# Moving the gathering tiles' scores ahead of the last four projections, and two tiles' routing beside them

## The chip, the cores and the metric

The kernel runs on one core of a Trainium2 chip. Its time is the device time of one execution in microseconds (us), taken as the median of several runs. Engines are named as the profile names them: PE is TensorE (PEld its weight loads), DVE is VectorE, ACT is ScalarE, POOL is GpSimd, SP is SyncE, whose queue issues most transfers.

## The reference, cut to what matters

One layer of an encoder over 1024 tokens of width 1024. A mixer (latent attention and a Hyena convolution) gives `mix`; after a layer norm, a PEER block picks 16 of 16384 experts for each of 8 heads of each token and sums their rows, weighted:

```
mix = concat([a, y]) @ w_o
h = layer_norm(ALPHA * h + mix)
# peer_ffn, for each chunk xc of 128 tokens:
q = (xc @ w_q).reshape(C, 8, 2, 64)
s = einsum('chpd,hpnd->chpn', q, sub_keys)       # 2 x 128 scores a head
sv, si = top_k(s, 16)                            # each half's best 16
cand = sv[:, :, 0, :, None] + sv[:, :, 1, None, :]
best, pos = top_k(cand, 16)                      # best 16 of their sums
eidx = take_along_axis(cidx, pos)                # expert numbers
g = softmax(best)
a = gelu(einsum('chkd,cd->chk', u_tab[eidx], xc))
f = einsum('chk,chkd->cd', g * a, v_tab[eidx])
h = layer_norm(ALPHA * h + f)
```

## The kernel before, in words

The 1024 tokens are 8 tiles of 128. The first NG = 3 tiles are gathering tiles: for them GpSimd fetches the chosen rows of both tables with indirect transfers, row by row (`gather`, L1233), and VectorE multiplies and sums them. The other DENSE = 5 tiles are dense tiles: TensorE multiplies them with the whole tables, 128 blocks of 128 experts, and a matrix of gates, built on chip (`build_g`), zeroes the experts that were not chosen.

The stages around the change, in program order:

- `mix(tt)` (L945) projects tile tt with `w_o`: ScalarE and VectorE split the operand into a high and a low half (`zh`, `zl`; two pairs of buffers, `first` and `second`), TensorE does 48 matmuls into two PSUM banks, VectorE adds the residual and normalises, and the tile is stored in `h2_d`. For the gathering tiles `transposed` puts the transposed halves in `hg` as soon as the next tile is projected.
- `scores(src, t0, nt)` (L971) makes the scores of nt tiles, head by head: the head's weight block `wr` and keys are loaded and split, TensorE projects (24 matmuls for each cut of the columns; the dense tiles have two cuts of 320) and multiplies with the keys, ScalarE copies, and `s_d` gets the result. It yields after each head.
- Before the change all 8 tiles are projected first. Then the gathering tiles' scores run, with the load and transposes of one dense tile (`hd`) after each of the first five heads; then the dense scores, with two pieces of `route(0)` after each head.
- `route(tt, rp, done)` (L1015) picks the experts of one tile from its scores. It is VectorE work, but for one Exp on ScalarE, in 11 pieces, and starts with a load of all of the tile's scores, `r_s` (L1019), into a pool whose tiles have one buffer each.
- The early u loop does 72 parts (`u_part`): 48 matmuls each on the dense tiles, an activation and a store in `a_d`. Its program also draws on `weights()`, a generator that yields the remaining routes and the five `build_g`: `route(NG)`, then each dense tile's `build_g` with the next tile's route beside it, then what is left. How much it draws for each part is set by `total`, and `tick` adds the gather's steps by a fixed rate.
- The main loop does the other 56 u parts, all v blocks and the rest of the gather.

What order the instructions take on each engine is planned when the kernel is built, with a simulated timeline (`schedule_with_timeline_sim=True` in `kernel`); each engine then works through its list in that order. `tc.issue_after(ins)` puts what is traced in its block behind `ins` on that engine. Pools opened with `side="right"` or `"left"` form two stacks in SBUF; a tile in a reopened space waits until the old tile's last reader is done.

Of the kernel before, what the change touches and what calls it, by code (L numbers as in the profile page):

```python
# [10 lines left out]
F32 = mybir.dt.float32  # L11
F32R = mybir.dt.float32r
# [9 lines left out]
P = 128  # L22
T = 1024
D = 1024
NT = T // P
ND = D // P
# [4 lines left out]
DENSE = 5  # L31
# [258 lines left out]
def split(nc, hi, lo, src):  # L290
    nc.scalar.copy(hi, src)  # L291
    return nc.vector.tensor_sub(lo, src, hi)  # L292
# [3 lines left out]
def layer(ctx: ExitStack, tc: tile.TileContext, a: dict, out: bass.AP):  # L296
    nc = tc.nc
    TD = DENSE * P
    NG = NT - DENSE
# [40 lines left out]
    def transposed(src, hi, lo, c0):  # L340

        for q in range(0, ND, 4):
            ps = psO.tile([P, 4, P], F32, name=f"ps_o{q // 4}")
            for ct in range(4):
                nc.tensor.transpose(ps[:, ct], src[:, (q + ct) * P:(q + ct + 1) * P], ident)
            r = split(nc, hi[:, q:q + 4, c0:c0 + P], lo[:, q:q + 4, c0:c0 + P], ps)
        return r

    s_mix = ExitStack()
# [525 lines left out]
    h2_d = dram.tile([NT, P, D], F32, name="h2_d")  # L875
    s_d = dram.tile([NT, P, 8, 256], F32, name="s_d")
    s_wo = ExitStack()
# [22 lines left out]
    n_h, n_a, done = 32, 72, 0  # L900
# [27 lines left out]
    s_q = ExitStack()  # L928
# [14 lines left out]
    normed = []  # L943
# [69 lines left out]
    CHUNK = 55.0 / 12  # L1013
# [96 lines left out]
    s_e = ExitStack()  # L1110
    with tc.tile_pool(name="hgp", bufs=1, side="right") as hgp:
        hg = hgp.tile([P, 2, ND, TG], F32R, name="hg")
        turn = None
        for tt in range(NT):
            m_t = mix(tt)
            if turn is not None:
                transposed(turn, hg[:, 0], hg[:, 1], (tt - 1) * P)
            turn = m_t if tt < NG else None
        s_wo.close()
        s_mix.close()  # L1120
        hdp = s_e.enter_context(tc.tile_pool(name="hdp", bufs=1, side="left"))
        hd = hdp.tile([P, 2, ND, TD], F32R, name="hd")
        with tc.tile_pool(name="hrp", bufs=2, side="left") as hrp:
            gs = scores(hg, 0, NG)
            for t in range(DENSE):
                next(gs)
                h_t = hrp.tile([P, D], F32, name="h_t")
                nc.sync.dma_start(h_t, h2_d[NG + t])
                transposed(h_t, hd[:, 0], hd[:, 1], t * P)
            for _ in gs:  # L1130
                pass


    CS = 32
# [3 lines left out]
    NB = 4  # L1138
    HOT = 0.69
# [155 lines left out]
    def tick(cost):  # L1295
        pace["credit"] += cost
        while pace["credit"] >= pace["step"]:
            pace["credit"] -= pace["step"]
            next(ga, None)
# [2 lines left out]
    n_steps = NG * (2 * P + GB)  # L1302
    pace["step"] = EARLY * UC / (n_steps * EHEAD)

    with tc.tile_pool(name="rp", bufs=1, side="left") as rp, \
            tc.tile_pool(name="gp", bufs=1, side="left") as gp:
        base = gp.tile([98, P], F32, name="base")
        own = gp.tile([98, 32], F32, name="own")
        nc.sync.dma_start(base, a["par_base"])
        nc.sync.dma_start(own, a["par_own"])  # L1310
        par_r = gp.tile([98, 32, P], BF16, name="par_r")
        nc.vector.tensor_mul(par_r, base.unsqueeze(1).to_broadcast([98, 32, P]),
                             own.unsqueeze(2).to_broadcast([98, 32, P]))
        jls = [gp.tile([98, 4, P], BF16, name=f"jl{i}") for i in range(2)]
        for jl in jls:
            nc.gpsimd.memset(jl[96:98], 1.0)
        r0 = route(0, rp, [])
        for _ in scores(hd, NG, DENSE):
            with tc.issue_after(normed[-1].ins):
                for _ in range(2):  # L1320
                    next(r0, None)
        for _ in r0:
            pass
        s_q.close()
        gap = s_e.enter_context(tc.tile_pool(name="gap", bufs=2, side="right"))

        def weights():


            done = []  # L1330
            yield from route(NG, rp, done)
            for t in range(DENSE):
                beside = route(NG + t + 1, rp, done) if t + 1 < DENSE else route(1, rp, done)
                for n, c in enumerate(build_g(done[t], t, gp)):
                    yield c
                    if n % 5 in (0, 2, 4):
                        yield next(beside, 0.0)
                yield from beside
            for g in range(2, NG):
                yield from route(g, rp, done)  # L1340

        gw = weights()
        total = (NT - 1) * 12 * CHUNK + TD // NB * HOT
        done = 0.0
        for e in range(EARLY):
            while done < (e + 1) * total / GFILL:
                c = next(gw, None)
                if c is None:
                    break
                done += c  # L1350
            A = u_part(e, u_early)
            nc.scalar.dma_start(a_d[e], A)
            tick(UC)
        for _ in gw:
            pass
# [199 lines left out]
```

## Time and profile before

| | |
|---|---|
| time, median of 3 runs | 3274.26 us (3264.43 to 3280.19) |
| the profiled execution's own time | 3255.75 us |
| its span in the profile | 3254.0 us |
| PE busy | 2988.5 us (92%) |
| DVE busy | 2735.7 us (84%) |
| ACT busy | 1256.2 us (39%) |
| POOL busy | 1036.4 us (32%) |
| mean granted clock of PE | 0.962 |

Busy times are sums over the whole span, and stages differ. The granted clock is a share of full speed: 1.00 is 2.4 GHz, and a lower mean is a mix of 2.4 and 1.2 GHz. Matmuls are pipelined, so the duration of one is longer than the distance to the next. The profiled execution is shorter than all three timed runs.

### The profile page before, as it was taken

The numbers are of one execution on the slowest core, as the hardware profiler recorded it, in microseconds if no ns is written. First come the engines' busy times: TensorE is split into PE (matmuls) and PEld (weight loads), VectorE is DVE, ScalarE is ACT, GpSimd is POOL, SyncE is SP. The second block draws the span as 40 slices with busy tenths as digits, with TensorE's granted clock in tenths as the row PEclk, the third lists the DMA queues.
The fourth block names the chain that finished last, engine by engine and source line by source line (L and its number), as shares of the span: only waits on it lengthen the run. The fifth ranks groups of instructions, "written<-read, shape, count | busy, mean of one in ns | idle before, by whom it ended". The sixth has DMA issues, their size and how long they took to land.

```text
span 3254.0 us, 44798 instructions
## 1 busy us (share of the span) xinstructions
PE 2988.5 (92%) x15582; PEld 2552.1 (78%) x15582; DVE 2735.7 (84%) x5514; ACT 1256.2 (39%) x2454; POOL 1036.4 (32%) x797
## 2 busy tenths in 40 slices
PE   6999898889999779999999789998999999799997
PEld 5677676556689778999898778886888888588886
DVE  7556799888757799999999768888889879888888
ACT  4544344455523216766574122222222222122222
POOL 0000000000000351332435735555555445455551
PEclk9999889989999989999999899999999999999998
DMA  5244743322444777887888999999999999989995
GB/s 173 97 149 133 249 123 104 102 56 73 138 152 149 278 252 241 302 303 277 310 284 319 364 338 336 325 358 341 329 358 323 353 315 333 337 302 353 342 332 188
DMA packets 355064, 828.87 MB, mean 255 GB/s; under 512 B 34345, under 2 KB 144851, under 8 KB 351253
## 3 DMA queue, kind: packets, MB, share of 16 engines
q0 software_dynamic: 110592, 402.70, 34.5%
q1 hardware_dynamic: 230709, 356.71, 33.9%
q10 hardware_dynamic: 13536, 66.59, 5.2%
q8 instruction: 123, 2.02, 0.2%
q14 instruction: 104, 0.85, 0.1%
HBM read 715.52 MB, written 110.33 MB: 254 GB/s over the span
## 4 chain that ended last, share of the span: by engine, by line
PE 31%; DVE 22%; DMA 7%; issue 6%; POOL 3%; ACT 1%; SPq 0%; DVEq 0%; POOLq 0%; ACTq 0%
PE ps_x L285 5%; PE ps_x L287 5%; PE ps_x L286 5%; DVE grow L1262 4%; DVE gacc L1270 4%; DMA vr<-in_peer_v 3%; PE ps_h L285 3%; PE ps_h L287 3%; PE ps_h L286 3%; POOL grow L1249 3%; DVE p L1160 2%; PE ps_o L285 2%; PE ps_o L286 2%; PE ps_o L287 2%; DVE ul L292 2%
## 5 line engine op out<-in xcount | busy, mean ns | idle before, releaser
L1249 POOL DMA_INDIRECT grow<-in_peer_u,eid x384 | 518.0, 1349 | 582.3 <-DVE grow L1262 206.9
L1249 POOL DMA_INDIRECT grow<-in_peer_v,eid x384 | 504.8, 1315 | 606.1 <-DVE gacc L1270 267.3
L1270 DVE SCALAR_TENSOR_TENSOR gacc<-grow,dot,gacc 128x1024 f32<-128x1024 f32 x381 | 487.3, 1279 | 13.2 <-DMA grow<-in_peer_v,eid 9.6
L1262 DVE SCALAR_TENSOR_TENSOR grow<-grow,gh 128x1024 f32<-128x1024 f32 x384 | 460.1, 1218 | 19.8 <-DMA grow<-in_peer_u,eid 19.5
L287 PE MATMUL ps_x<-hd,ul 128*128 128x320 f32 x1152 | 368.3, 328 | 50.1 <-DVE ul L292 49.7
L285 PE MATMUL ps_x<-hd,uh 128*128 128x320 f32 x1152 | 373.6, 325 | 28.4 <-ACT uh L291 26.2
L286 PE MATMUL ps_x<-hd,uh 128*128 128x320 f32 x1152 | 370.3, 322 | 0.0
L286 PE MATMUL ps_x<-vl,wh 128*128 128x512 f32 x864 | 341.1, 395 | 1.7 <-DVE vl L292 1.6
L287 PE MATMUL ps_x<-vh,wl 128*128 128x512 f32 x864 | 336.8, 393 | 0.0
L285 PE MATMUL ps_x<-vh,wh 128*128 128x512 f32 x864 | 302.3, 396 | 28.4 <-ACT vh L291 23.2
L291 ACT CAST vh<-vr 128x512 fp32r<-128x512 f32 x256 | 156.3, 619 | 388.4 <-DMA vr<-in_peer_v 280.6
L285 PE MATMUL ps_h<-hd,uh 128*128 128x320 f32 x896 | 278.8, 311 | 9.0 <-ACT A L1221 5.6
L286 PE MATMUL ps_h<-hd,uh 128*128 128x320 f32 x896 | 278.3, 311 | 0.0
L287 PE MATMUL ps_h<-hd,ul 128*128 128x320 f32 x896 | 275.8, 311 | 2.5 <-DVE ul L292 2.5
L287 PEld LDWEIGHTS ps_x<-hd,ul 128*128 128x128 f32 x1152 | 222.7, 195 | 65.0 <-DVE ul L292 59.0
L285 PEld LDWEIGHTS ps_x<-hd,uh 128*128 128x128 f32 x1152 | 225.9, 196 | 35.4 <-ACT uh L291 31.8
L292 DVE TENSOR_TENSOR vl<-vr,vh 128x512 fp32r<-128x512 f32 x256 | 174.5, 687 | 75.7 <-ACT vh L291 74.4
L286 PEld LDWEIGHTS ps_x<-hd,uh 128*128 128x128 f32 x1152 | 225.8, 196 | 0.8
L291 ACT CAST uh<-ur 128x1024 fp32r<-128x1024 f32 x128 | 134.7, 1052 | 223.7 <-DMA ur<-in_peer_uT 103.1
L285 PEld LDWEIGHTS ps_x<-vh,wh 128*128 128x128 f32 x864 | 162.7, 190 | 63.5 <-ACT vh L291 24.7
L292 DVE TENSOR_TENSOR ul<-ur,uh 128x1024 fp32r<-128x1024 f32 x128 | 155.5, 1215 | 63.8 <-ACT uh L291 62.4
L286 PEld LDWEIGHTS ps_x<-vl,wh 128*128 128x128 f32 x864 | 164.4, 190 | 37.1 <-DVE vl L292 4.4
(366 smaller groups left out, 6876.3 us busy)
## 6 DMA issues: line engine op xcount, KB each, us to landing
ur<-in_peer_uT SPq DMA_DIRECT2D x128, 512.0 KB
vr<-in_peer_v SPq DMA_DIRECT2D x256, 256.0 KB
g_d<-gst ACTq DMA_DIRECT2D x20, 2048.0 KB
gt<-g_d SPq DMA_DIRECT2D x32, 1280.0 KB
a_d<-A ACTq DMA_DIRECT2D x72, 320.0 KB
A<-a_d SPq DMA_DIRECT2D x72, 320.0 KB
fw<-in_dft_fw SPq DMA_DIRECT2D x64, 256.0 KB
wr<-in_w_in SPq DMA_DIRECT2D x16, 512.0 KB
```

The lines of the kernel that those rows point to most:

```text
L285: nc.tensor.matmul(out, L[0], R[0], start=start, stop=False)
L286: nc.tensor.matmul(out, L[0], R[1], start=False, stop=False)
L287: return nc.tensor.matmul(out, L[1], R[0], start=False, stop=stop)
L291: nc.scalar.copy(hi, src)
L292: return nc.vector.tensor_sub(lo, src, hi)
L1160: nc.vector.tensor_tensor(p1, iota.unsqueeze(1).to_broadcast([P, NB, P]), ig[:, 0, c:c + NB].unsqueeze(2).to_broadcast([P, NB, P]), op=ALU ...
L1249: nc_i = nc.gpsimd.indirect_dma_start(out=t, out_offset=None, in_=a["peer_" + kind], in_offset=bass.IndirectOffsetOnAxis(ap=eid[g][:, k:k ...
L1262: nc.vector.scalar_tensor_tensor(t, t, 1.0, h_t, op0=ALU.mult, op1=ALU.mult, accum_out=d[:, k - k0:k - k0 + 1])
L1270: nc.vector.scalar_tensor_tensor(acc, t, dots[k0][:, k - k0:k - k0 + 1], acc, op0=ALU.mult, op1=ALU.add)
```

## The change

The gathering tiles' scores are made as soon as four tiles are projected. Then a pool `rp0` is opened on the right, in the space that `hg` leaves, and two routes, of tiles 0 and 1, are chained in one generator, `r0`. Two of its pieces are traced after each of the four projections that are left, one after the transposes of each dense tile, and two after each head of the dense scores; there are 22 in all. The dense transposes no longer have the gathering scores between them. `weights()` has route(2) where route(1) was, and `total` counts one route less. The pools `rp` and `gp`, and the table `par_r`, now come after the dense scores.

```diff
-        for tt in range(NT):
+        for tt in range(NG + 1):
             m_t = mix(tt)
             if turn is not None:
                 transposed(turn, hg[:, 0], hg[:, 1], (tt - 1) * P)
-            turn = m_t if tt < NG else None
-        s_wo.close()
-        s_mix.close()
-        hdp = s_e.enter_context(tc.tile_pool(name="hdp", bufs=1, side="left"))
-        hd = hdp.tile([P, 2, ND, TD], F32R, name="hd")
-        with tc.tile_pool(name="hrp", bufs=2, side="left") as hrp:
-            gs = scores(hg, 0, NG)
-            for t in range(DENSE):
-                next(gs)
-                h_t = hrp.tile([P, D], F32, name="h_t")
-                nc.sync.dma_start(h_t, h2_d[NG + t])
-                transposed(h_t, hd[:, 0], hd[:, 1], t * P)
-            for _ in gs:
-                pass
+            turn = m_t
+        for _ in scores(hg, 0, NG):
+            pass
+    rp0 = s_q.enter_context(tc.tile_pool(name="rp0", bufs=1, side="right"))
+    r0 = (c for g in range(2) for c in route(g, rp0, []))
+    for tt in range(NG + 1, NT):
+        mix(tt)
+        for _ in range(2):
+            next(r0)
+    s_wo.close()
+    s_mix.close()
+    hdp = s_e.enter_context(tc.tile_pool(name="hdp", bufs=1, side="left"))
+    hd = hdp.tile([P, 2, ND, TD], F32R, name="hd")
+    with tc.tile_pool(name="hrp", bufs=2, side="left") as hrp:
+        for t in range(DENSE):
+            h_t = hrp.tile([P, D], F32, name="h_t")
+            nc.sync.dma_start(h_t, h2_d[NG + t])
+            transposed(h_t, hd[:, 0], hd[:, 1], t * P)
+            next(r0, None)
...
+    for _ in scores(hd, NG, DENSE):
+        with tc.issue_after(normed[-1].ins):
+            for _ in range(2):
+                next(r0, None)
+    for _ in r0:
+        pass
+    s_q.close()
+    gap = s_e.enter_context(tc.tile_pool(name="gap", bufs=2, side="right"))
     with tc.tile_pool(name="rp", bufs=1, side="left") as rp, \
             tc.tile_pool(name="gp", bufs=1, side="left") as gp:
...
-        r0 = route(0, rp, [])
-        for _ in scores(hd, NG, DENSE):
-            with tc.issue_after(normed[-1].ins):
-                for _ in range(2):
-                    next(r0, None)
-        for _ in r0:
-            pass
-        s_q.close()
-        gap = s_e.enter_context(tc.tile_pool(name="gap", bufs=2, side="right"))
...
-                beside = route(NG + t + 1, rp, done) if t + 1 < DENSE else route(1, rp, done)
+                beside = route(NG + t + 1, rp, done) if t + 1 < DENSE else route(2, rp, done)
...
-            for g in range(2, NG):
+            for g in range(3, NG):
                 yield from route(g, rp, done)
...
-        total = (NT - 1) * 12 * CHUNK + TD // NB * HOT
+        total = (NT - 2) * 12 * CHUNK + TD // NB * HOT
```

## Rows read from the trace of the kernel before

**Rows 1.** The page: span, and busy time of each engine.

```profile
span 3254.0 us, 44798 instructions
PE 2988.5 (92%) x15582; PEld 2552.1 (78%) x15582; DVE 2735.7 (84%) x5514; ACT 1256.2 (39%) x2454; POOL 1036.4 (32%) x797
```

**Rows 2.** Busy time by stage: stretch, length, engines, granted clock, DMA share, GB/s.

```profile
897.00:940.00 43.00, 43.00 (x196) 35.72 (x195) 26.22 (x39) 4.74 (x10) 0.00 (x0) 1.00 0.24 86
940.00:992.00 52.00, 52.00 (x310) 50.67 (x310) 22.58 (x26) 24.45 (x43) 0.99 (x2) 1.00 0.67 222
992.00:1067.00 75.00, 73.54 (x461) 70.74 (x460) 55.59 (x233) 26.36 (x51) 0.00 (x0) 1.00 0.39 125
1067.00:1250.00 183.00, 139.31 (x842) 134.36 (x841) 173.85 (x664) 45.57 (x83) 79.49 (x58) 0.89 0.77 264
1250.00:1750.00 500.00, 475.48 (x3356) 456.24 (x3355) 497.31 (x1448) 326.49 (x900) 163.58 (x129) 0.98 0.83 293
1750.00:1838.00 88.00, 73.24 (x460) 69.05 (x459) 72.98 (x79) 24.71 (x54) 56.42 (x40) 0.94 0.94 355
1838.00:3254.00 1416.00, 1332.16 (x6759) 1160.83 (x6757) 1203.67 (x1623) 365.30 (x603) 723.30 (x542) 0.98 0.93 328
```

**Rows 3.** TensorE's timeline, 938 to 952: start, length, instruction.

```profile
939.58 0.40 PE L287 MATMUL ps_x<-wo,zl 128*128 128x512 f32 x1
...
945.88 1.04 PE L345 MATMUL ps_o<-ident,h_t 128*128 128x128 f32 x8
```

**Rows 4.** Busy time by stage of L1221, two halves a u part.

```profile
1067.00:1250.00 183.00, 18.78 (x37) 0.89 0.77 264
1250.00:1750.00 500.00, 44.07 (x89) 0.98 0.83 293
1750.00:1838.00 88.00, 7.08 (x17) 0.94 0.94 355
```

**Rows 5.** Waits in 1067 to 1670: total us, times, longest.

```profile
PE ps_x L287 <- DVE ul L292: 43.5, 15, 7.3
```

**Rows 6.** VectorE's timeline, 990 to 1072; in brackets the idle time before.

```profile
992.41 4.43 DVE L1312 TENSOR_TENSOR par_r<-base,own 98x4096 bf16<-98x4096 f32 x1 [3.85 <-DMA own<-in_par_own]
...
1001.83 1.26 DVE L1023 MAX8 r_sv<-r_s 128x8 f32<-128x128 f32 x6 [3.86 <-DMA r_s<-s_d]
...
1017.29 1.21 DVE L292 TENSOR_TENSOR wl<-wr,wh 128x1024 fp32r<-128x1024 f32 x1
...
1051.98 0.23 DVE L1078 CAST eid<-r_ef 128x128 int32<-128x128 f32 x1
1071.62 1.23 DVE L292 TENSOR_TENSOR ul<-ur,uh 128x1024 fp32r<-128x1024 f32 x1 [19.42 <-ACT uh L291]
```

**Rows 7.** VectorE's instruction groups, 1001 to 1053: busy us, mean ns.

```profile
L292 DVE TENSOR_TENSOR wl<-wr,wh 128x1024 fp32r<-128x1024 f32 x5 | 6.1, 1215 | 0.0
```

**Rows 8.** ScalarE's timeline, 940 to 1090.

```profile
1004.19 1.05 ACT L291 CAST wh<-wr 128x1024 fp32r<-128x1024 f32 x1 [1.94 <-PE ps_x L286]
```

**Rows 9.** The chain that ended last, 985 to 1110.

```profile
993.65 0.38 ACT sc L999
994.05 2.75 DMA s_d<-sc
996.86 4.95 DMA r_s<-s_d
```

**Rows 10.** SP's timeline of issued transfers, 855 to 1140.

```profile
940.05 0.80 SPq L1128 DMA_DIRECT2D h_t<-h_d  x2
...
996.86 0.33 SPq L1019 DMA_DIRECT2D r_s<-s_d  x1
```

**Rows 11.** TensorE's instruction groups, 860 to 1067: busy us, mean ns.

```profile
L345 PE MATMUL ps_o<-ident,h_t 128*128 128x128 f32 x40 | 5.2, 273 | 0.0
```

**Rows 12.** TensorE's timeline, 1300 to 1322: two matmuls in a row.

```profile
1299.96 0.31 PE L287 MATMUL ps_x<-hd,ul 128*128 128x320 f32 x1
1300.11 0.31 PE L285 MATMUL ps_x<-hd,uh 128*128 128x320 f32 x1
```

## The prediction

> **What bounds the kernel now.** I read the page's busy shares first [rows 1]: TensorE 92%, VectorE 84% of 3254.0 us. An average over unlike stages decides nothing, so the table by stage comes next [rows 2]. I chose its cuts from the timelines: 897–940 is the projection of the last four tiles (its last matmul is at 939.58 [rows 3]); 940–992 the gathering tiles' scores with the dense tiles' transposes between them; 992–1067 the dense scores with route(0) beside them; 1067–1838 the early u loop, whose 72 parts write two halves each (143 of 144 lie in it [rows 4]), with the other seven routes, build_g and the gather's first steps; 1838–3254 the main loop.
>
> The reader should see two things. Up to 1067 TensorE is full: 43.0 of 43, 52.0 of 52, 73.5 of 75 us, while VectorE has room: 26.2, 22.6 and 55.6 us. From 1067 it turns round: VectorE is busy 744.1 us of 771 (173.85 + 497.31 + 72.98, 96.5%), TensorE 688.0 (89%). In 1250–1750 they stand at 497.3 and 475.5 of 500. The waits of the early loop say the same: matmuls wait 43.5 us for the low half of a u block, which VectorE makes [rows 5]. The main loop holds no instruction that changes and moves as a whole with what comes ahead of it.
>
> **Part 1: one route leaves the early loop.** Before, route(1) and route(2) lie in it beside five dense routes; after, only route(2). Route(0) shows the price: its first instruction starts at 1001.83, its last ends at 1052.21 [rows 6], and in these 50.4 us stand five weight splits of 6.1 us [rows 7]: 44.3 us, or 4.03 for each of its 11 pieces. `total` falls with it, so the rest is still spread over the loop.
>
> How much is the loop shortened by 44.3 us less VectorE work? At VectorE's present share of 96.5% the other 699.8 us take 725 us: a gain of 46. At that length TensorE's 688 us would be 95%, as high as it stands now in 1250–1750. This is the upper end. For the lower end I let TensorE hold the middle: the outer stretches (271 of 771 us) take their part of the saving, 44.3 × 271/771 = 15.6 us, and the middle gains half of TensorE's 24.5 idle us, 12.3: together 28. I take 38, a little above the midpoint of 37, since TensorE at 733 us is at 94%, not above what the middle shows already.
>
> A page speaks on this room. The row first: in 1250–1750 weight loads are busy 456.2 us, 91.2%, against 50.67 of 52 (97.4%) where matmuls run back to back in 940–992 [rows 2]. The Trainium skill, Perfetto Trace Analysis, section Identifying the Most-Contended Engine, says to judge TensorE by weight-load share, not by matmul time. By it the middle's room would be an estimated 500 × (1 − 0.912/0.974) = 32 us, and the lower end 31 instead of 28.
>
> **Part 2: routes 0 and 1 beside the last four projections.** TensorE's instructions are the same; only their order and cover change. Two pieces follow each of four mixes: 8 pieces, 32.2 us, where VectorE has 43 − 26.2 = 16.8 us free. What is queued behind them on VectorE: the next tile's splits, then its residual add, which frees the PSUM banks; TensorE waits for both. A queue of this kind is there already: a weight block's cast ends at 1005.24 and its split starts only at 1017.29, 12 us later, behind route pieces that the program emits first [rows 8, 6]. There TensorE had other heads to do and lost 1.5 us in 75. So the upper end is 32.2 − 16.8 = 15 us; the lower end is 0, because two operand pairs and four banks let TensorE run a tile (43/4 = 10.8 us) ahead. I take 8, midway.
>
> The route also starts later than TensorE's next tile: from the last score copy at 993.65 the store takes 2.75 and the load 4.95 us until VectorE starts at 1001.83, 8.2 us [rows 9]. The load waits in SP's queue for that store [rows 10]; behind it stand the projections' h_t loads and h2_d stores, which have a tile's lead over 8.2 us. I cost this at nothing; without the lead it is 8.2 us, about half of the 15. The second load waits for route(0)'s last read of its one buffer; behind it stand dense weight loads with two buffers, cost nothing, the bound again one landing, 5 us. The gathering scores' 8 weight loads, 16 key loads and 8 stores move past four mixes' loads and stores on SP; in 897–940 transfers hold 24% of the engines [rows 2], so they find room. Exp in a route needs ScalarE, 26.4 of 75 us busy beside the dense scores: nothing. The 4.43 us par_r product [rows 6] moves behind the dense scores; VectorE stands idle 19.42 us ahead of 1071.62 [rows 6], which hides it; without that it is 4.4 us. GpSimd's first gather still waits for the end of the scores.
>
> **Part 3: the dense transposes lose their cover.** This is what is late next. The second mix tail is not new, but in 940–992 the gathering scores filled it: TensorE 52.0 of 52. After the change those scores are done by then. The first two h_t loads go out at 940.05, with the last matmul of the projections, and the first transposes run at 945.88 [rows 10, 3]: 5.8 us. Two buffers for five tiles make three turns. Tiles 0 to 2, which the first half of a head's columns needs, are in place after about 5.8 + 1.0 + 5.8 us and a transpose and its split, some 16 us, of which TensorE works 3 (40 transposes took 5.2 us [rows 11]): 13 lost. While the last tiles come, two heads' first halves (24 matmuls at 0.147 us [rows 12], 3.5 us each) fill in. With landings of 4 us (between the 2.75 and 4.95 of [rows 9]) it is 10: the lower end. The upper end adds route pieces that stand ahead of the splits, 4 × 4.03 = 16 more: 29. I take 15, near the unburdened chain, since VectorE has free time while the loads land.
>
> **Part 4: the clock.** The granted clock is 1.00 (2.4 GHz) in all of 897–1067, where TensorE never rests, and 0.89, a mix of 2.4 and 1.2 GHz, in 1067–1250, where it idles 43.7 us [rows 2]. There 0.11 × 183 = 20 us of full speed go with 43.7 idle, 0.46 for each; by the same ratio 13 idle us cost 6. Lower end 0; I take 3. The Trainium skill, TensorE: Matmul & The Clock Gate, section HAM oscillation, has the rule that speaks against this change: after a gap TensorE's clock is cut and the next matmuls start slow. By that rule the sum would be 3 us worse than the one below, by an unmoved clock 3 better; the low clock of 1067–1250 agrees with the rule.
>
> **Sum.** −38 + 8 + 15 + 3 = −12 us. The profiled execution took 3255.75 us, so 3244 by its own time. It lies 18.5 us below the median of 3274.26 (three runs, 3264.43 to 3280.19), so against the median: 3262. The ends: −46 + 10 = −36 and −28 + 15 + 29 + 6 = +22. A difference of 0.5%, 16.4 us, is about what a measurement of this kernel can tell from none.
>
> **The rivals.**
> *The routes hide* (chance 0.22). The pieces run in VectorE's idle time, as they do beside the dense scores, where 44.3 us of route cost TensorE 1.5. Front 10, loop −46: −36, 3238. For it: VectorE has 16.8 + 19.4 free us and the order on each engine is planned when the kernel is built. Against it: two routes are 88.6 us, and from the gathering scores' end TensorE has 43 + 5 + 75 = 123 us left, of which the route loses 8.2 to the landing and VectorE gives 26 to the mixes and more to the splits: nothing may slip.
> *TensorE is the floor* (0.10). The loop gives 28 only: −28 + 26 = −2, 3272. For it: 475.5 of 500 in the middle. Against: the first 183 us have 43.7 us idle on TensorE.
> *The route queue stops the projections* (0.18), the one that ends slower. The place is VectorE's queue between the first and the last projection after the scores: pieces are taken in program order, the next tile's split behind them. If none of the 8 pieces hides, the mixes lose 32 and the tail its upper 29: 61 + 3 against 38, +26, 3300. It decides from a front loss of 38 + 16.4 = 54 on. For it: the 12 us of [rows 8, 6]. Against: that split waited without hurting, since TensorE had a lead.
> That the change does not put the routes there at all, because the planner leaves them to the dense scores, is a form of the first: mixes cost 0, the tail 13, loop −38: −25, 3249.
>
> **How the numbers follow.** My forecast, −12, has 0.50; its own range is 3247 to 3281, and of its half I put 0.20 past −16.4, 0.27 within, 0.03 above. The first rival adds 0.20 to faster and 0.02 to same, the second 0.10 to same, the third 0.18 to slower. Faster 0.40, same 0.39, slower 0.21. The range reaches down past the first rival's 3238 by its landings, to 3232, and up to 3292, short of the queue's 3300: what is left out is most of that 0.18.
>
> **What the profile after would show.** Part 1: the stretch from the end of the dense scores to the 72nd u part at some 733 us, with six routes in it (6 × 16 first MAX8, before 7 × 16), VectorE still above 95% and TensorE near 94%. Part 2: MAX8 of route(0) between the projection's residual adds, and matmuls of the last two projections waiting for zl splits some 8 us in all. Part 3: a TensorE gap of 10 to 15 us ahead of the first dense score matmul, ended by an hd split or an h_t load; the dense scores ending 20 to 30 us later than 1067. Part 4: a granted clock below 1.00 in the first dense heads. The prediction is wrong if the dense scores end before 1080 with the loop at 725, or after 1120, or if the early loop is not shorter than 760.

## The result and the profile after

The kernel after the change takes 3349.43 us (median of 4 runs, 3348.02 to 3352.83) against 3269.35 us for the kernel before beside it (3256.91 to 3280.19): a ratio of 1.0258, 95% interval 1.0237 to 1.0278. It is 80 us slower, outside the predicted range of 3232 to 3292.

The page of the kernel after (span, then busy time of each engine), which answers to [rows 1]:

```profile
span 3346.3 us, 44821 instructions
PE 3029.9 (91%) x15582; PEld 2574.8 (77%) x15582; DVE 2734.8 (82%) x5514; ACT 1252.6 (37%) x2452; POOL 1044.4 (31%) x797
```

VectorE's total work is the same as before, within a microsecond; the span is 92.3 us longer (more than the medians' 80, since the profiled execution of before lies 13.6 us below its median). To split it I use three marks: the first residual add of the projections, the last score copy, and the store of the 72nd u part. The stores are read from the rows of `a_d` (instruction, count, min/median/max ns, first and last start), first of the kernel before:

```profile
L1352 ACTq DMA_DIRECT2D a_d<-A x72: 326/326/356, 1072.0 to 1887.1; - x72
```

and of the kernel after:

```profile
L1355 ACTq DMA_DIRECT2D a_d<-A x72: 325/326/336, 1103.1 to 1973.7; - x72
```

The dense scores end at 1067.0 before and 1098.1 after, 5 us ahead of the first store. The early loop runs from there to the last store.

| stretch | before | after | difference |
|---|---|---|---|
| up to the first residual add | 870.6 | 873.1 | +2.5 |
| front, to the end of the dense scores | 196.3 | 225.0 | +28.7 |
| early loop | 820.1 | 875.6 | +55.5 |
| the rest | 1366.9 | 1372.5 | +5.6 |

So the front cost what I had forecast (26 us). The loop, which was to gain 38, lost 55.5. The rows of stages answer to [rows 2] (stretch, length, busy time of PE, PEld, DVE, ACT, POOL, granted clock, DMA share, GB/s). The whole loop of before:

```profile
1067.00:1887.00 820.00, 726.46 (x4883) 695.58 (x4882) 782.23 (x2237) 405.49 (x1049) 335.77 (x254) 0.95 0.83 297
```

The kernel after: the front behind the gathering scores, the start of the loop, its last two stretches, and all of it:

```profile
948.00:1098.00 150.00, 130.92 (x707) 117.80 (x706) 130.20 (x507) 38.06 (x71) 0.99 (x2) 0.92 0.35 117
1098.00:1281.00 183.00, 140.99 (x804) 135.39 (x804) 173.26 (x657) 43.40 (x79) 72.07 (x59) 0.85 0.77 266
1750.00:1901.00 151.00, 129.22 (x809) 117.43 (x808) 112.99 (x144) 73.66 (x210) 84.44 (x65) 0.91 0.92 343
1901.00:1974.00 73.00, 68.93 (x444) 68.13 (x445) 19.49 (x19) 21.58 (x33) 3.83 (x3) 0.95 0.49 167
1098.00:1974.00 876.00, 759.88 (x4896) 717.27 (x4896) 755.16 (x2025) 403.91 (x1052) 344.36 (x260) 0.92 0.80 283
```

VectorE has 27 us less to do in the loop (seven gathered rows more are used in it, 256 against 249) and stands idle 121 us of it, against 38 before. Near the end neither engine is full (1750 to 1901), and in the last 73 us VectorE has 19.5 us of work. The waits around the u blocks in the loop, before (waiting instruction, what it waited for, us in total, times, longest):

```profile
ACT uh L291 <- DMA ur<-in_peer_uT: 81.8, 26, 11.7
DVE ul L292 <- ACT uh L291: 27.8, 6, 19.4
PE ps_x L287 <- DVE ul L292: 49.7, 23, 7.3
DVE p L1160 <- PE ps_h L1183: 0.8, 1, 0.8
```

and after:

```profile
ACT uh L291 <- DMA ur<-in_peer_uT: 149.5, 28, 11.3
DVE ul L292 <- ACT uh L291: 74.2, 18, 13.4
PE ps_x L287 <- DVE ul L292: 67.1, 27, 7.5
DVE p L1165 <- PE ps_h L1188: 22.5, 18, 7.5
```

The first three lines are one chain. The third answers to [rows 5], here over the whole loop. A u block is loaded into `ur`, which has one buffer; ScalarE casts it (`uh`), VectorE subtracts (`ul`), and only then may the next block's load go out. The fourth line is VectorE's wait for a build's matmul. One long u part of the kernel after shows how it locks. ScalarE's timeline (start, us, engine, line; in brackets the idle time before it and what ended it):

```profile
1859.67 0.44 ACT L1226 ACTIVATE A<-ps_x 128x320 f32<-128x320 f32 x1 [2.78 <-PE ps_x L287]
1860.14 0.33 ACTq L1355 DMA_DIRECT2D a_d<-A  x1
1860.56 0.59 ACT L1189 COPY gst<-ps_h 128x512 f32<-128x512 f32 x1 [0.45 <-PE ps_h L1188]
1861.04 1.15 ACT L1171 ACTIVATE p<-ps_o,ig 128x128 f32<-128x128 f32 x4
1862.06 0.61 ACT L1189 COPY gst<-ps_h 128x512 f32<-128x512 f32 x1
...
1868.43 1.37 ACT L1171 ACTIVATE p<-ps_o,ig 128x128 f32<-128x128 f32 x4
1869.45 1.29 ACT L291 CAST uh<-ur 128x1024 fp32r<-128x1024 f32 x1
1870.38 0.47 ACT L1270 ACTIVATE dot<-dot 128x16 f32<-128x16 f32 x1
1870.50 0.83 ACT L1189 COPY gst<-ps_h 128x512 f32<-128x512 f32 x1
...
1879.50 0.33 ACTq L1355 DMA_DIRECT2D a_d<-A  x1
```

VectorE's, GpSimd's and SyncE's:

```profile
1848.94 1.22 DVE L292 TENSOR_TENSOR ul<-ur,uh 128x1024 fp32r<-128x1024 f32 x1
...
1860.56 0.69 DVE L1165 TENSOR_TENSOR p<-iota,ig 128x512 f32<-128x512 f32 x1 [7.51 <-PE ps_h L1188]
...
1870.77 1.23 DVE L292 TENSOR_TENSOR ul<-ur,uh 128x1024 fp32r<-128x1024 f32 x1
```

```profile
1862.67 1.15 POOL L1254 DMA_INDIRECT grow<-in_peer_v,eid  x1 [7.57 <-DVE grow L1267]
```

```profile
1850.18 0.33 SPq L1207 DMA_DIRECT2D ur<-in_peer_uT  x1
```

From store to store (1860.14 to 1879.50) this part takes 19.4 us. Nine build steps stand in it in ScalarE's list, about 1.48 us apart, and the next block's cast has its place behind the sixth; its split follows at 1870.77, 21.8 us after the one before. The block's load goes out at 1850.18, as soon as the split before it is done, and the cast shows no wait for it: in this part it is the cast's place in ScalarE's list that holds the next block. While TensorE does the u part's matmuls from 1850.21 on, VectorE stands 7.51 us before a builder of one-hot rows that needs a build's matmul to be over, gathered rows queue behind it, and GpSimd waits 7.57 us for those. While the builds run, the next u part waits for its split. The stages take turns instead of running side by side.

### The profile page after: what moved, and what is told of

Read it like the earlier page. It is cut to its first block, busy times and chain, and to the rows that moved or that the text cites. A ratio compares the mean times of both kernels' runs of the same rounds, so it can differ in the third digit from the quotient of the medians.

```text
span 3346.3 us, 44821 instructions
## 1 busy us (share of the span) xinstructions
PE 3029.9 (91%) x15582; PEld 2574.8 (77%) x15582; DVE 2734.8 (82%) x5514; ACT 1252.6 (37%) x2452; POOL 1044.4 (31%) x797
## 5 line engine op out<-in xcount | busy, mean ns | idle before, releaser
L1254 POOL DMA_INDIRECT grow<-in_peer_u,eid x384 | 526.9, 1372 | 572.6 <-DVE grow L1267 179.0
L287 PE MATMUL ps_x<-hd,ul 128*128 128x320 f32 x1152 | 373.5, 333 | 67.1 <-DVE ul L292 67.1
L285 PE MATMUL ps_x<-hd,uh 128*128 128x320 f32 x1152 | 379.0, 330 | 31.5 <-ACT uh L291 31.4
L286 PE MATMUL ps_x<-hd,uh 128*128 128x320 f32 x1152 | 374.8, 326 | 0.0
L287 PEld LDWEIGHTS ps_x<-hd,ul 128*128 128x128 f32 x1152 | 230.5, 202 | 77.6 <-DVE ul L292 76.2
L285 PEld LDWEIGHTS ps_x<-hd,uh 128*128 128x128 f32 x1152 | 233.3, 203 | 39.9 <-ACT uh L291 38.3
L286 PEld LDWEIGHTS ps_x<-hd,uh 128*128 128x128 f32 x1152 | 232.4, 202 | 0.5
```

Of the source, the lines that this page charges most:

```text
L285: nc.tensor.matmul(out, L[0], R[0], start=start, stop=False)
L286: nc.tensor.matmul(out, L[0], R[1], start=False, stop=False)
L287: return nc.tensor.matmul(out, L[1], R[0], start=False, stop=stop)
L1254: nc_i = nc.gpsimd.indirect_dma_start(out=t, out_offset=None, in_=a["peer_" + kind], in_offset=bass.IndirectOffsetOnAxis(ap=eid[g][:, k:k ...
```

## The experiments

The program draws on routes and builds by its own units of cost, spread over GFILL = 71 parts: before 495.4, 6.98 a part; after 440.4, 6.20 a part, because `total` counts a route less. Front, loop and rest are those of the profiled execution, as in the table above; "long" is the number of u parts of 15 us and more, from the 72 stores.

| kernel | routes in loop | units a part | front | loop | rest | long | ratio to before |
|---|---|---|---|---|---|---|---|
| before | 7 | 6.98 | 196.3 | 820.1 | 1366.9 | 9 | 1 |
| after | 6 | 6.20 | 225.0 | 875.6 | 1372.5 | 18 | 1.0258 (1.0237 to 1.0278) |
| 1: loop only | 6* | 6.20 | 202.6 | 860.2 | 1349.5 | 16 | 1.0027 (1.0009 to 1.0045) |
| 2: front only | 7 | 6.98 | 217.2 | 825.0 | 1372.3 | 9 | 1.0076 (1.0048 to 1.0103) |
| 3: after, old count | 6 | 6.98 | 226.8 | 836.4 | 1362.2 | 11 | 1.0081 (1.0054 to 1.0108) |
| 4: after, 2 buffers | 6 | 6.20 | 227.0 | 717.0 | 1420.6 | 4 | 0.9912 (0.9890 to 0.9935) |
| 5: before, 2 buffers | 7 | 6.98 | 199.6 | 723.4 | 1436.8 | 2 | 0.9890 (0.9848 to 0.9931) |
| 6: before, low count | 7 | 6.20 | 196.7 | 858.1 | 1369.8 | 17 | 1.0122 (1.0085 to 1.0160) |
| 7: 4 with old count | 6 | 6.98 | 224.5 | 723.0 | 1403.7 | 5 | 0.9871 (0.9848 to 0.9895) |
| 8: 1 with 2 buffers | 6* | 6.20 | 201.5 | 724.4 | 1416.2 | 4 | 0.9832 (0.9805 to 0.9859) |
| 9: 8 with old count | 6* | 6.98 | 201.7 | 737.8 | 1422.7 | 3 | 0.9871 (0.9852 to 0.9889) |
| 10: before, drawn faster | 7 | 7.99 | 195.8 | 869.7 | 1378.5 | 16 | 1.0167 (1.0149 to 1.0185) |
| 11: 8 drawn faster | 6* | 7.86 | 202.2 | 761.2 | 1407.8 | 7 | 0.9947 (0.9930 to 0.9964) |
| 12: after, norm loads moved | 6 | 6.20 | 223.8 | 869.5 | 1357.0 | 19 | 1.0190 (1.0162 to 1.0219) |
| 13: before, the same | 7 | 6.98 | 196.8 | 840.3 | 1354.4 | 10 | 0.9998 (0.9978 to 1.0017) |
| 14: 8, the same | 6* | 6.20 | 201.3 | 731.7 | 1407.3 | 3 | 0.9833 (0.9810 to 0.9856) |
| 15: after, gather faster | 6 | 6.20 | 225.3 | 869.3 | 1364.3 | 15 | 1.0245 (1.0213 to 1.0278) |
| 16: after, gather slower | 6 | 6.20 | 226.4 | 849.8 | 1377.3 | 11 | 1.0184 (1.0154 to 1.0213) |

\* In these runs the second route is not done when the dense scores end: its expert numbers are cast 74 to 76 us into the loop, so part of a seventh route's work is still there.

A profiled execution can lie some 10 us off its median, and the stretch up to the first residual add, the same code in all 18, ends between 860.6 and 877.4 us; so I tell single loops apart from about 15 us on.

**Runs 1 to 3: the parts of the change by themselves.** Run 1 is the kernel before with

```diff
-        r0 = route(0, rp, [])
+        r0 = (c for g in range(2) for c in route(g, rp, []))
...
-                for _ in range(2):
+                for _ in range(3):
                     next(r0, None)
```

and the change's own edits of `weights` and `total`.

> The kernel before, with the loop of the kernel after: routes 0 and 1 are chained beside the dense scores (three pieces a head), six routes are left in the early loop, and the draw on them counts six. The order of projections, scores and transposes is that of before. If the loop follows VectorE's work, as the prediction had it, it ends some 38 us earlier (820 us from the end of the dense scores to the store of the 72nd part become 782), the front gives back at most 10, and the time is about 3240 us. If the loop is set by the way its work is spread over the 72 parts (a smaller count draws more slowly: builds end at part 63 in place of 60), or by the chain of load, cast and split of one u block after the other, one route less shortens nothing: 820 to 876 us, and a time of 3270 to 3330. If the whole loss of the kernel after came in by its front (a later start, a lower clock), this loop is no longer than before, 3230 to 3270.

Measured: 3276.93 against 3262.91 us. One route less, drawn at the new rate, lengthened the loop by 40 us; the second route beside the dense scores cost the front 6.3. The rest is 17 us shorter, so the time rose by 0.27% alone. The reading that all of the loss comes in by the front has fallen. On VectorE's work this run says less than I wanted, because the second route reaches into the loop; the cast of its expert numbers, and the whole loop:

```profile
1148.97 0.22 DVE L1078 CAST eid<-r_ef 128x128 int32<-128x128 f32 x1
1075.30:1935.40 860.10, 748.16 (x4899) 708.00 (x4898) 777.10 (x2069) 407.75 (x1054) 350.78 (x260) 0.94 0.80 289
```

VectorE is busy 777.1 us in it, only 5 less than before. Runs 2 and 3 below settle that question.

Run 2 is the kernel after with

```diff
-    r0 = (c for g in range(2) for c in route(g, rp0, []))
+    r0 = route(0, rp0, [])
...
         mix(tt)
-        for _ in range(2):
-            next(r0)
...
-            next(r0, None)
```

and `weights` and `total` as before.

> The kernel after, without the second route ahead of the loop: gathering scores behind four tiles' projection, dense transposes without scores between them, route(0) beside the dense scores alone as before, route(1) back in the loop and in its count. If the loss comes from the loop's share of work and its spread, only the tail is left: 10 to 29 us, 3280 to 3298 in all, with a loop of about 820 us. If the changed front spoils the loop by itself, the loop stays near 876 us and the time near 3340.

Measured: 3290.06, +0.76%, with a loop of 825.0. The new order of projections, scores and transposes costs 20.9 us in the front and leaves the loop alone, within what one profile can tell.

Run 3 is the kernel after with one line of before:

```diff
-        total = (NT - 2) * 12 * CHUNK + TD // NB * HOT
+        total = (NT - 1) * 12 * CHUNK + TD // NB * HOT
```

> The kernel after with one number changed: the count that sets the draw holds seven routes again, as before, though six are left. Routes and builds are drawn faster, the last of them at about part 63 of 72, builds end near part 55 to 60. If the slower draw made the loop long, the loop comes back to 780 to 830 us and the time to 3260 to 3300. If the chain of load, cast and split of one u block paces the loop whatever the draw, the loop stays at 850 to 880 and the time at 3330 to 3350.

Measured: 3292.94, +0.81%; the loop fell from 875.6 to 836.4. The one number holds 56 of the 80 us. What stays, 30 us over the kernel before, is the size of the front's loss (30.5 in this profile).

Runs 2 and 3 have the same order of projections, scores and transposes and the same draw; one route less lies in the loop of run 3. Their loops, run 2 first:

```profile
1084.00:1909.00 825.00, 725.96 (x4869) 694.98 (x4867) 783.06 (x2237) 402.34 (x1047) 329.43 (x254) 0.95 0.82 296
1102.00:1939.00 837.00, 735.74 (x4898) 699.89 (x4897) 754.90 (x2025) 404.28 (x1052) 347.02 (x260) 0.95 0.82 296
```

VectorE has 28 us less to do and the loop is 11 us longer, not 28 to 46 shorter. So the reading by VectorE's work has fallen.

**Run 4: a second landing buffer** in the kernel after, used by every other u block of the early loop:

```diff
-    loads = []
+    loads, spare = [], []
...
-        ur = up.tile([P, ND, P], F32, name="ur", bufs=1)
+        p, n = (spare[0], "ur2") if spare and i % 2 else (up, "ur")
+        ur = p.tile([P, ND, P], F32, name=n, bufs=1)
...
+        spare.append(gp)
...
+        spare.clear()
```

> The kernel after with a second landing buffer for u blocks during the early loop (every other block lands in it), so that a block's load need not wait for the split of the block before. If that chain paces the loop, the casts' wait for loads (131.6 us in 22 waits between 1100 and 1700 us) shrinks to under 40 us and the loop falls from 876 towards VectorE's 755 us of work and its present waits for builds and gathered rows: 790 to 830, a time of 3270 to 3310. If the spread of the work or the order on VectorE's queue sets it, the waits move elsewhere and the loop stays at 860 to 880, the time at 3335 to 3350.

Measured: 3235.54, faster than the kernel before by 0.9%. Its loop:

```profile
1100.00:1817.00 717.00, 693.90 (x4889) 677.44 (x4888) 683.62 (x1942) 402.33 (x1046) 266.67 (x206) 0.98 0.83 303
```

TensorE is busy 97% and VectorE 95%; no cast waits for a u block's load any more, VectorE waits 24.8 us for casts in place of 74.2, and TensorE 20.2 for splits in place of 67.1:

```profile
DVE ul L292 <- ACT uh L291: 24.8, 8, 12.5
PE ps_x L287 <- DVE ul L292: 20.2, 5, 8.2
```

The loop fell by 159 us, further than either theory had it. Part of that comes back: 203 gathered rows are used in it in place of 256, and the rest grows by 48 us. The Trainium skill, Perfetto Trace Analysis, section Optimization Strategy, says that a gap which repeats on the engine that should be saturated can mean that there are too few buffers for the next tile; here the trace agrees, by these 159 us.

**Runs 5 to 8: the same, crossed.** Run 5 is the kernel before with the buffer of run 4.

> The kernel before with the second landing buffer for u blocks, seven routes in the loop. With the second buffer in the kernel after, the loop took 717 us with TensorE at 97% and VectorE at 95%, so both are near their work there. If VectorE's work sets the length once the chain is gone, the seventh route adds some 38 us to that loop, 755, and the front saves 29: about 3245, 5 to 15 above the kernel after with the same buffer. If TensorE sets it, the loop is 717 to 725 and the time 3205 to 3220. If the second buffer only cures what the kernel after does wrong, the loop stays near 820 and the time near 3263.

Measured: 3227.08. The loop of 723.4 is as TensorE's bound had it, with seven routes as with six; the time is 7 us above that forecast, since the rest is the longest of all, 1436.8, with 190 rows used in the loop.

Run 6 is the kernel before with

```diff
-        total = (NT - 1) * 12 * CHUNK + TD // NB * HOT
+        total = (NT - 2) * 12 * CHUNK + TD // NB * HOT
```

> The kernel before with one number changed: the count that sets the draw holds six routes although seven are drawn, so that builds come later by the same ratio as in the kernel after. Front and work are those of before. If the slower draw is what makes the loop long, the builds end at about part 67 to 69 of 72, the loop grows from 820 to 840 to 880 us and the time to 3285 to 3320. If the draw does not matter and the front of the kernel after did it, the time stays at 3255 to 3270.

Measured: 3303.08, +1.22%; the loop is 38 us longer with the front untouched and the same routes and builds in it, and the long parts go from 9 to 17. Its loop in the table by stage:

```profile
1067.00:1926.00 859.00, 749.33 (x4912) 710.63 (x4911) 796.29 (x2251) 410.06 (x1055) 339.26 (x260) 0.93 0.81 290
```

Run 7 is run 4 with the count of run 3.

> The kernel after with the second landing buffer and with the count at seven routes. If the draw mattered only through the chain of load, cast and split, the two edits do not add: 3230 to 3240, as with the buffer alone (3235.5). If the draw is a cost of its own (the loop's builds last until part 70 there), the loop falls from 717 to 690 to 700, TensorE's own 680 to 694 being the floor, and the time to 3210 to 3225.

Measured: 3220.31. The gain over run 4 is there, but not in the loop (723.0). In the profiled executions the rest is 17 us shorter, with as many gathered rows used (204), and 11 us lie ahead of the first residual add, where the two kernels are the same. The mechanism that I had named for it is wrong.

Run 8 is run 1 with the second buffer: the order of before, two routes beside the dense scores, six in the loop.

> The order of before, routes 0 and 1 beside the dense scores, six routes in the loop, and the second landing buffer. The front costs 6 to 8 us (measured with one buffer), the loop has the work of the kernel after. If the loop's length with two buffers depends on its work alone, it is 717 us as with the changed front, and the time is 3235 less some 22: about 3213. If VectorE is no bound even there, it equals the kernel before with the second buffer within 8 us.

Measured: 3208.77, the fastest of all, 1.7% faster than the kernel before. It stands 27 us ahead of run 4, which differs by the change's front, and 18 ahead of run 5, which differs by where one route stands and by the count. What the route is worth by itself doesn't follow from this: run 9 below has the count of run 5.

**Runs 9 to 11: other draws.** Run 9 is run 8 with `total` at (NT - 1); run 10 the kernel before, run 11 run 8, with GFILL (the parts over which the draw is spread) at 62 and 56 in place of 71.

> The order of before with routes 0 and 1 beside the dense scores, six routes in the loop, the second landing buffer, and the count at seven routes. In the kernel after with two buffers this count gave 15 us (3235.5 to 3220.3), and the changed front cost 27 (3235.5 against 3208.8). If the two add, 3190 to 3200; if the draw gained only where the changed front had made the loop late, 3205 to 3212.

> The kernel before, one buffer, seven routes, drawn faster still: over 62 parts in place of 71, so 8.0 units of the program's own cost for each part where before has 7.0 and the kernel after 6.2. The loop took 858 to 876 us in three kernels with 6.2 units and 820 to 836 in three with 7.0, whatever their routes. If a slower draw lengthens the loop because builds are left for its end, a faster one shortens it further or leaves it: 790 to 820, 3230 to 3263. If 7.0 is where the loop is best balanced, and any other draw bunches the work, it is 830 to 860, and 3275 to 3305.

> As the run with the order of before, six routes and two landing buffers (3208.8), drawn over 56 parts in place of 71: 7.9 units for each part. With two buffers TensorE is at 97% of the loop, so a faster draw can't shorten the loop below some 700 us; what it can do is to leave the last parts to the gather, whose steps then stand ahead in the main loop. If that pays, 3190 to 3205; if the faster draw bunches builds, the loop grows past 730 and the time is 3209 to 3230.

Measured: 3224.24, 3318.08, 3246.13. In run 9 the two gains didn't add; it is 15 us slower than run 8, which neither expectation had. It is 3 us from run 5, which has the same draw and order and the second route in the loop: at that draw, moving part of the route is worth nothing that can be told from none. Runs 10 and 11 came out slower than either range had. Run 10 tells most: drawn faster, the loop of before is 50 us longer, though its builds end at part 54. My theory that a slower draw is bad because builds are left to the end has fallen. The kernel before stands at a draw from which both directions lose.

**Runs 12 to 14: the loads of the last norm.** In the kernel after GpSimd waits 98.2 us where the first tile's gather ends (34.6 in the kernel before):

```profile
2007.93 1.86 POOL L1254 DMA_INDIRECT grow<-in_peer_u,eid  x1 [98.25 <-DVE gacc L334]
```

The norm's two loads stand in SyncE's queue behind u blocks' loads and the main loop's first ones, and go out at 1999.74. The edit, in the kernels after, before and of run 8:

```diff
-            nc.sync.dma_start(t, bcast(a[n]))
+            nc.gpsimd.dma_start(t, bcast(a[n]))
```

> The kernel after, with the two loads that end each gathering tile (gains and offsets of the last norm) issued by GpSimd, behind the gather's own loads, in place of SyncE, where they stand behind the u blocks' loads of the main loop. In the kernel after GpSimd waits 98.2 us there, and the last eight u parts have no gathered row beside them. If this wall is where the freed VectorE time is lost, the second tile's gather starts in the early loop, over 256 gathered rows are used in it, the main loop's 1372 us fall by some 1.1 us for each row more (as between the kernels with two landing buffers), and the time falls by 30 to 60 us, to 3290 to 3320. If the loss is in the bunches of builds and the chain of u blocks alone, the wait goes but the time stays at 3335 to 3355.

> The kernel before with the same two loads issued by GpSimd. There GpSimd waits 34.6 us at that place and gathered rows stand beside every u part to the end of the early loop. If the wall is the loss of the kernel after, there is a third of it to be had here: 5 to 20 us, 3245 to 3260. If moving the loads does anything else than open the wall (a slower issue, another planned order), this one shows it: 3265 or more.

> The order of before, routes 0 and 1 beside the dense scores, six routes in the loop and two landing buffers (3208.8), with the same two loads issued by GpSimd. With two buffers the loop ends after some 207 gathered rows of 256, so no wall is met in it: 3200 to 3215 by either theory. A time below 3195 would say that the wall costs in the main loop too.

Measured: 3325.19, 3259.22, 3209.32. Run 12 gives 24 us back, which lies between its two expectations, but GpSimd still waits there, now for VectorE to use a row of the second tile:

```profile
1999.04 1.68 POOL L1254 DMA_INDIRECT grow<-in_peer_u,eid  x1 [94.44 <-DVE grow L1267]
```

VectorE's own list has no row of the second tile in the early loop; 256 rows are used, as before the edit. Where the 24 us come from (the rest is 15.5 shorter) is not settled, since moving the loads gave every engine a new order. Run 13 gives nothing that can be told from none (0.9998), against 5 to 20 us expected, and run 14 is run 8 again.

**Runs 15 and 16: closing that hole.** EHEAD, the share of the gather's steps traced beside the early loop, at 0.34 and at 0.24 in place of 0.28, in the kernel after.

> The kernel after with one number changed, the share of the gather's steps that is traced beside the early loop: 0.34 in place of 0.28. In VectorE's list of the kernel after, the first tile's last gathered row stands before the 64th block's split and the second tile's first one behind the 78th; in this kernel's list second-tile rows follow from the 68th block on. If that hole in the list is where the time goes, over 256 rows are used in the early loop and the time falls by 30 to 60 us, to 3290 to 3320. If bunches of builds between lone u parts are the loss, the loop keeps its 18 parts of 15 us and more, and the time is 3335 to 3355; the steps drawn faster can even cost.

> The kernel after with that share at 0.24 in place of 0.28: the gather's steps are drawn more slowly, and VectorE's list has the first tile's last row before the 69th block's split and goes on with second-tile rows from the 72nd. If the hole at the loop's end is the loss, it closes here too: 3290 to 3320. If bunches of builds are, 3335 to 3355, or more by what the gather now does later (32 steps fewer in the early loop, some 35 us in the main loop).

Measured: 3340.54 and 3323.07. In run 15, 297 rows are used in the loop and gathered rows stand beside its last parts, and yet the loop is 6 us and the rest 8 us shorter: closing the hole is worth little here. Run 16, the slower draw of the gather, uses 279 rows and closes it too; it does better, with 11 long parts and a loop of 849.8, and its time lies between the two expectations. What run 16 has beyond the closed hole was not separated.

## Why the prediction was wrong

**Part 1 is the step that failed.** "At VectorE's present share of 96.5% the other 699.8 us take 725 us" turns a busy share into a length. The loop does not follow VectorE's work. At 6.98 units a part it takes 820 and 825 us with seven routes and 836 with six; at 6.20 it takes 858 with seven, 860 with six and part of a seventh, and 876 with six. The pair that isolates the route, runs 2 and 3, gives +11 for 28 us less work. The term of -38 measured +55.5. Of this, 39 is `total` (run 3; the converse, run 6, gives 38), and the 16 that are left to run 3 are about what two profiled loops can differ by. The bounds of -28 to -46 left out a loss, because I costed "`total` falls with it, so the rest is still spread over the loop" at nothing. That sentence was the expensive one.

**What the runs showed in its place.** With one landing buffer the loop is a chain of load, cast and split, in lists whose order is fixed when the kernel is built. Its length depends on how builds, gathered rows and u blocks fall beside each other: with one buffer the loops of up to 840 us have 9 to 11 parts of 15 us and more, those from 849 on 11 to 19. The second buffer takes most of that away: runs 4, 5, 7, 8, 9 and 14, with six or seven routes, either front and 6.20 or 6.98 units a part, lie at 717 to 738. That the lower draw costs what it does only with the single buffer is shown by the pairs: with one buffer 875.6 and 836.4 (after and run 3), with two 717.0 and 723.0 (runs 4 and 7) and 724.4 and 737.8 (runs 8 and 9). A draw of 7.86 costs with two buffers too (761, run 11). The buffer also changes the planned order, so how much of its gain is the casts' 149.5 us of waits for loads, and how much the new places of casts and builds, isn't separated. Why just these draws bunch the work, and why both a slower and a faster one do, was not shown: each edit gives the planned order of all engines anew.

**The end of the loop was misread.** I took 1838 from a count of activations [rows 4], 143 of 144; that group also holds loads of the activation table, and only 67 of the 72 stores lie ahead of 1838. The last one is at 1887.1. With the right end VectorE's share is 95.4% (782.2 of 820), so the sum would have been the same in kind. The Trainium skill, Perfetto Trace Analysis, section Identifying the Most-Contended Engine, takes occupancy as a fair measure of how near VectorE is to its limit. In the loop of before it was 95.4% and in that of run 2 94.9%, and the work that run 3 takes away made the loop no shorter: there the measurement decides, and a high occupancy did not make VectorE the bound in a loop with a chain of single buffers. The section Optimization Strategy, cited at run 4, was the better guide.

**Parts 2 to 4, the front: 26 forecast, 28.7 measured.** TensorE's waits behind the gathering scores (waiting instruction, what ended the wait, total, times, longest):

```profile
PE ps_o L345 <- DVE hd L292: 7.2, 5, 2.6
PE ps_o L345 <- DMA h_t<-h_d: 6.4, 1, 6.4
PE ps_x L287 <- DVE zl L292: 2.1, 1, 2.1
PE ps_x L286 <- DVE hd L292: 2.1, 1, 2.1
PE ps_x L285 <- ACT hd L291: 0.7, 1, 0.7
```

The mixes waited 2.1 us for a split, not 8: at this place the planned order lets the pieces fill in. The tail lost 7.2 + 6.4 + 2.1 + 0.7 = 16.4, with 15 forecast. The size is right, the reason only in part: 6.4 is the wait for a landing, but 7.2 + 2.1 are waits for splits. I had counted on VectorE's free time there, and it has none; route pieces stand between the splits:

```profile
1000.00:1025.00 25.00, 17.88 (x89) 15.29 (x90) 25.00 (x131) 7.18 (x13) 0.00 (x0) 0.67 0.26 85
```

That is the term that I had put into the upper end alone, so the match is partly luck. TensorE's idle time from 948 to 1098 is 19.1 us, and 0.08 of 150 us at full speed, 12, went with the lower clock, some of it in that idle time. So the clock's 3 was too small: of the 28.7, all but the idle time (19.1, less the 1.5 that these stages had before) is 11. The granted clock is 0.67 between 1000 and 1025, among the transposes, behind the wait of 6.4 us. The Trainium skill, TensorE: Matmul & The Clock Gate, section HAM oscillation, has the clock cut after a gap and what follows start slow. The trace agrees, and speaks for more than I gave it. Run 2 splits the front: 20.9 us for the order with one route, whose pieces the plan puts among the transposes there too, and the other 8 for the second route.

**The rivals.** "The route queue stops the projections" came nearest in sign, but not in place: the front loss is half of the 54 from which it decides. "The routes hide" was right in the mixes and useless. "TensorE is the floor" came near the truth only with two buffers. No rival held that the loop itself could get longer. Of the signs of being wrong that I had named, a loop not shorter than 760 is the one that came.

## What to carry to other kernels

A high busy share of an engine that works through a fixed list doesn't make it the bound; where a single-buffered chain runs through it, take some of its work out in a run, or give the chain a second buffer, before work is moved for its sake. A pacing constant that is worked out from the amount of work is an edit of its own: here it held 56 us of 80, while the route that it stands for shortened the loop by nothing (825 and 836 us at the same draw). Compare at the same constant, too. The fastest kernel (run 8, 3209 us) has two buffers, the lower count and a front that left the transposes covered, but how much of its 18 us over run 5 is the moved route isn't shown: at the higher count the same move gave 3 (run 9). At the lower count with one buffer it gave 26 (run 6 to run 1, 3303 to 3277 us) with the loops alike (858 and 860): in the profiles the rest is 20 us shorter, and why stays open.

## What the runs showed of the hardware

TensorE's clock came down in short stops inside the loop. In the part above, TensorE had stood 2.74 us for a split. Its timeline:

```profile
1850.21 0.63 PE L287 MATMUL ps_x<-hd,ul 128*128 128x320 f32 x1 [2.74 <-DVE ul L292]
```

The stretches ahead of the wait, from this matmul on, and after, in the table by stage:

```profile
1832.00:1850.00 18.00, 14.93 (x105) 13.20 (x103) 13.58 (x22) 13.79 (x41) 10.39 (x9) 0.98 0.99 389
1850.20:1856.30 6.10, 6.09 (x23) 6.09 (x24) 2.85 (x5) 0.00 (x0) 2.62 (x2) 0.50 1.03 413
1856.30:1859.50 3.20, 3.20 (x24) 3.20 (x23) 0.00 (x0) 0.44 (x1) 0.00 (x0) 1.00 0.66 253
```

The granted clock is 0.50 (1.2 GHz) for 6.1 us and 1.00 (2.4 GHz) afterwards; 23 matmuls take 6.1 us and the next 24 take 3.2. So a wait of some 3 us cost another 3 at half speed. The loop's mean clock is 0.95 before and 0.92 after. With the second buffer it is 0.98, and TensorE is busy 693.9 us in place of 759.9 for as many matmuls (4889 and 4896): 66 of the 159 us by which run 4 shortened the loop.
